# A two-layer attention and feed-forward kernel: a new order of work at the entry into the attention stages

## The chip, the cores and the metric

The kernel runs on one core of a Trainium2 chip. The metric is the device time of one execution in microseconds (us), as the median of several runs. Beside it stands one profiled execution, whose trace gives every instruction of the five engines with its start and length: TensorE (PE; its weight loads as PEld), VectorE (DVE), ScalarE (ACT), GpSimd (POOL) and SyncE (SP, which only issues transfers).

## The reference

Two layers over a sequence of 256 tokens and 1024 features, in float32. Cut to what matters:

```python
for l in range(2):
    h = rmsnorm(x, norm_mix_g[l])                      # mean of squares over 1024 features
    a_qkv, b_q, b_kv, b_gate, merge = split(h @ w_in[l])
    out_a = dilated_mixer(rope(rmsnorm(qa)), rope(rmsnorm(ka)), va)   # 24 heads, three dilations
    k_cmp, v_cmp = compress(...)                       # blocks of 32 tokens, gelu(flat @ w1) @ w2
    out_b = nsa_mixer(rope(rmsnorm(qb)), k_cmp, v_cmp, k_sel, v_sel, k_win, v_win, b_gate)
    gate = sigmoid(merge)
    x = x + (gate_a * (out_a @ w_proj_a[l]) + gate_b * (out_b @ w_proj_b[l])) @ w_out[l]
    h = rmsnorm(x, norm_ffn_g[l])
    g, u = split(h @ w_up[l])                          # 2816 each
    x = x + (silu(causal_dwconv(g, conv_w[l], conv_b[l])) * u) @ w_down[l]
```

The mean of squares is not needed ahead of the products with `w_in` and `w_up`: 1/rms is one factor a token, and the kernel applies it to the results.

## The kernel before

**Units.** All weights come as one stream of units of 128 x 2048 float32 in the order of use. A unit arrives in two halves of 512 KB (`load_half`, L206 on, five buffers `raw`), and each half is split in two parts: ScalarE casts it to `hi` (L238), VectorE subtracts to get `lo` (L239), and every product is three matmuls, hi x hi, lo x hi, hi x lo (`mm3`, L290 to L292; L373 and others in the feed-forward part). So TensorE can begin a half only after ScalarE and VectorE have been through it.

**Entry.** At the start (from L1093) SP issues x in the permuted token order (`xo`, three pieces), the gains and the first two units, interleaved. `feed` (L305 on) scales each of eight 128-feature tiles of x by the gain into a hi and a lo part (ACT L310, DVE L311) and squares it; at the start the first four squares are made by GpSimd (L323), the others by ScalarE (L325), and GpSimd adds them up (L329). VectorE makes the last sum `fin` (L333). The same function feeds the later stages from `x`, where all squares are ScalarE's.

**First three chunks of an attention stage.** `chunk_in` multiplies h by 512 (or 280) columns of `w_in`, in two units (halves kh of the 1024 features) and two token halves t, into two PSUM buffers `acc` of three. The first chunk, `c10`, has the compressed keys and values and half of the others, `c11` (280 columns) the rest and the gates, `bq` the queries. Between the two token halves of `c10`'s second unit stands `rstd_col` (L341 on): two matmuls with `ones` sum `fin` over the features, VectorE scales, GpSimd takes the power -0.5 (L347), VectorE writes two diagonals `dg` (L351). Only with rstd can ScalarE read a chunk out of PSUM, `scaled` (L419): `craw`, `kraw`, `vB`. Each group of heads then runs through `rope_run`, a generator that is stepped by `tick()` between groups of matmuls: squares, sums (L427), power on GpSimd (L378), rotation on VectorE with the tables `tabs` (L436, L437, L440), and `fin`, which copies and transposes (`rd`, L482 and L485). GpSimd makes the tables from `cossin` and `gr` (two instructions at L394, one for `tabc` at L397).

`job_cmp1` (from L787) prepares the compressed blocks: VectorE duplicates (`cdup`, L792), TensorE transposes with the identity (L795), ScalarE copies out of PSUM in natural token order, eight copies a layer (`T`, L802), VectorE adds position terms (`F`, L810). It is begun by a tick inside `c11`.

**Behind the entry.** Nine more chunks follow with the attention steps between them (`job_a`, `job_b`), then projections, and the feed-forward part, where the first unit's matmuls of both output tiles are interleaved, `rstd_col` stands before its 43rd matmul and the row form of rstd before the 25th of the second unit.

**Order.** The code is written as one sequence; a scheduler of the framework sets the final order on each engine's queue, and each engine runs its queue in order.

## Time and profile before

| | |
|---|---|
| median of three runs | 968.22 us (965.47 to 968.27) |
| the profiled execution | 964.59 us |
| its span, first to last instruction | 962.8 us |
| TensorE busy | 936.6 us (97%) |
| VectorE busy | 753.0 us (78%) |
| ScalarE busy | 580.2 us (60%) |
| GpSimd busy | 154.7 us (16%) |
| read from memory | 163.69 MB |

An instruction's row gives its start, its length, the engine, the line, what it writes and reads, and in brackets how long its engine had been idle before it and what ended that. Matmuls overlap: the distance between two starts says what one costs, not its length. The attention stages run from the start to about 240 us and from 484 to about 720 us, the feed-forward parts behind them.

### The profile page before, as it was taken

The numbers are of one execution on the slowest core, as the hardware profiler recorded it, in microseconds if no ns is written. First come the engines' busy times: TensorE is split into PE (matmuls) and PEld (weight loads), VectorE is DVE, ScalarE is ACT, GpSimd is POOL, SyncE is SP. The second block draws the span as 40 slices with busy tenths as digits, with TensorE's granted clock in tenths as the row PEclk, the third lists the DMA queues.
The fourth block names the chain that finished last, engine by engine and source line by source line (L and its number), as shares of the span: only waits on it lengthen the run. The fifth ranks groups of instructions, "written<-read, shape, count | busy, mean of one in ns | idle before, by whom it ended". The sixth has DMA issues, their size and how long they took to land.

```text
span 962.8 us, 18575 instructions
## 1 busy us (share of the span) xinstructions
PE 936.6 (97%) x7122; PEld 848.9 (88%) x7122; DVE 753.0 (78%) x1595; ACT 580.2 (60%) x1186; POOL 154.7 (16%) x179
## 2 busy tenths in 40 slices
PE   6899999999999999999998999999999999999998
PEld 4778887878999999999986787877799999999998
DVE  6898866887679889986478987678876888998742
ACT  6778665666556555555456986466755555655431
POOL 6140211212002111110122301122200111111000
PEclk9999999999999999999999999999999999999999
DMA  7734446525456565666455344554354465666660
GB/s 242 255 132 155 150 157 207 189 88 174 148 162 213 180 210 187 189 196 204 147 168 174 112 151 135 196 196 140 121 180 153 161 217 175 205 197 203 196 209 19
DMA packets 48041, 165.95 MB, mean 172 GB/s; under 512 B 6096, under 2 KB 7632, under 8 KB 47824
## 3 DMA queue, kind: packets, MB, share of 16 engines
q1 hardware_dynamic: 46800, 163.71, 52.1%
q8 instruction: 56, 0.92, 0.4%
q10 hardware_dynamic: 1152, 1.05, 0.3%
q14 instruction: 33, 0.27, 0.1%
HBM read 163.69 MB, written 1.05 MB: 171 GB/s over the span
## 4 chain that ended last, share of the span: by engine, by line
PE 78%; DVE 10%; ACT 6%; issue 2%; POOL 1%; DMA 1%; SPq 0%; DVEq 0%; ACTq 0%; POOLq 0%
PE acc L373 25%; PE acc L290 5%; PE acc L292 5%; PE acc L291 5%; DVE lo L239 4%; PE acc L1082 4%; PE acc L1084 4%; PE acc L1083 4%; PE acc L957 3%; PE att L571 3%; PE acc L959 3%; PE acc L958 3%; PE att L576 2%; PE acc L993 2%; PE acc L994 2%
## 5 line engine op out<-in xcount | busy, mean ns | idle before, releaser
L239 DVE TENSOR_TENSOR lo<-raw,hi 128x1024 fp32r<-128x1024 f32 (+1 forms) x292 | 368.4, 1279 | 51.6 <-ACT hi L238 49.4
L238 ACT CAST hi<-raw 128x1024 fp32r<-128x1024 f32 (+1 forms) x292 | 294.0, 1037 | 150.9 <-PE acc L291 36.9
L373 PE MATMUL acc<-u,hi 128*128 128x256 f32 x1376 | 236.3, 277 | 0.0
L373 PEld LDWEIGHTS acc<-u,hi 128*128 128x128 f32 x1376 | 207.4, 188 | 0.1
L373 PE MATMUL acc<-u,lo 128*128 128x256 f32 x688 | 190.2, 276 | 0.0
L290 PE MATMUL acc<-hi,hT 128*128 128x512 f32 (+1 forms) x384 | 154.0, 401 | 8.7 <-ACT hi L238 8.7
L292 PE MATMUL acc<-lo,hT 128*128 128x512 f32 (+1 forms) x384 | 150.0, 391 | 5.2 <-DVE lo L239 5.1
L291 PE MATMUL acc<-hi,hT 128*128 128x512 f32 (+1 forms) x384 | 148.5, 387 | 0.0
L373 PEld LDWEIGHTS acc<-u,lo 128*128 128x128 f32 x688 | 129.1, 188 | 0.0
L1084 PE MATMUL acc<-act,lo 128*128 128x256 f32 x352 | 97.2, 276 | 0.0
L1082 PE MATMUL acc<-act,hi 128*128 128x256 f32 x352 | 97.2, 276 | 0.0
L1083 PE MATMUL acc<-act,hi 128*128 128x256 f32 x352 | 97.2, 276 | 0.0
L290 PEld LDWEIGHTS acc<-hi,hT 128*128 128x128 f32 x384 | 72.6, 189 | 25.9 <-ACT hi L238 11.1
L292 PEld LDWEIGHTS acc<-lo,hT 128*128 128x128 f32 x384 | 72.4, 189 | 23.6 <-DVE lo L239 9.2
L291 PEld LDWEIGHTS acc<-hi,hT 128*128 128x128 f32 x384 | 72.7, 189 | 12.6 <-issue 0.3
L957 PE MATMUL acc<-hT,hi 128*128 128x256 f32 x256 | 73.4, 287 | 0.0
L959 PE MATMUL acc<-hT,lo 128*128 128x256 f32 x256 | 71.8, 281 | 0.0
L958 PE MATMUL acc<-hT,hi 128*128 128x256 f32 x256 | 71.7, 280 | 0.0
L1084 PEld LDWEIGHTS acc<-act,lo 128*128 128x128 f32 x352 | 66.1, 188 | 0.0
L1082 PEld LDWEIGHTS acc<-act,hi 128*128 128x128 f32 x352 | 66.1, 188 | 0.0
L1083 PEld LDWEIGHTS acc<-act,hi 128*128 128x128 f32 x352 | 66.1, 188 | 0.0
L1054 POOL TENSOR_TENSOR z<-z,rb 128x512 f32<-128x512 f32 x22 | 30.5, 1386 | 203.1 <-DVE z L1053 203.1
(215 smaller groups left out, 1690.2 us busy)
## 6 DMA issues: line engine op xcount, KB each, us to landing
raw<-in_ws_dram SPq DMA_DIRECT2D x300, 512.0 KB, 4.6
raw<-in_ws_dram SPq DMA_DIRECT2D x8, 280.0 KB, 4.2
x<-in_x_dram SPq DMA_DIRECT2D x1, 1024.0 KB, 9.6
out_dram<-x ACTq DMA_DIRECT2D x8, 128.0 KB, 2.7
gr<-in_g_rope_dram SPq DMA_DIRECT2D x2, 384.0 KB, 4.4
masks<-in_mask_dram SPq DMA_DIRECT2D x1, 576.0 KB, 7.6
xo<-in_xo_dram SPq DMA_DIRECT2D x2, 256.0 KB, 4.5
xo<-in_xo_dram SPq DMA_DIRECT2D x1, 512.0 KB, 7.0
```

Of the source, the lines that this page charges most:

```text
L238: A.copy(h, r)
L239: V.tensor_sub(l, r, h.bitcast(F32))
L290: T.matmul(o, a_hi, b_hi, start=first, stop=False)
L291: T.matmul(o, a_lo, b_hi, start=False, stop=False)
L292: T.matmul(o, a_hi, b_lo, start=False, stop=last)
L373: return [lambda a=a: T.matmul(a[0], a[1], a[2], start=a[3], stop=a[4]) for a in todo]
L957: T.matmul(o, hi[:, k, ms], hT[:, 0, k], start=k == 0, stop=False)
L958: T.matmul(o, hi[:, k, ms], hT[:, 1, k], start=False, stop=False)
L959: T.matmul(o, lo[:, k, ms], hT[:, 0, k], start=False, stop=k == 7)
L1082: T.matmul(ps, hi[:, c], act[:, 0, k], start=k == 0, stop=False)
L1083: T.matmul(ps, hi[:, c], act[:, 1, k], start=False, stop=False)
L1084: T.matmul(ps, lo[:, c], act[:, 0, k], start=False, stop=k == NFT - 1)
```

## The change

It rearranges the entries. At the start x and the gains are issued from ACT's queue, the first unit comes in quarters of 256 KB on SP's, each cast and subtracted by itself, and `c10`'s first unit is multiplied quarter by quarter for both token halves. Fourteen matmuls of `ones` with itself, whose result nobody reads, stand first on TensorE. The squares of the first x are made by ScalarE for two tiles at once and added by VectorE; GpSimd has none. In all four places `rstd_col` writes the diagonals with ScalarE; in the attention stages it stands behind all of `c10`, in the feed-forward parts at the fourth matmul of the second unit. In `c11` the token half is the outer loop. The tables are made in pieces, those that the keys need first; `job_cmp1` starts behind `c11`, transposes with two permuted identities, so that the copies out of PSUM are in natural order and two per head pair suffice. The copy `rd` is made before the wait that precedes its transposes and has two buffers of its own.

```diff
+    idle = att()
+    for i in range(14):
+        T.matmul(idle[:, 0:P], ones, ones, start=True, stop=True)
...
-            for c0 in (0, w // 2):
+            step = w // 4 if (i, w // 4) in early else w // 2
+            for c0 in range(0, w, step):
...
+        if src is not x:
+            if m % 2:
+                sq = com.tile([P, 2, S], F32, name="sq2", bufs=2)
+                A.activation(sq, src[:, m - 1:m + 1], AF.Square)
+                if m > 1:
+                    V.tensor_add(sq, sq, sums["acc"])
+                sums["acc"] = sq
+            if m == 7:
+                sums["fin"] = com.tile([P, S], F32, name="fin", bufs=1)
+                V.tensor_add(sums["fin"], sq[:, 0], sq[:, 1])
+            return
...
-            V.tensor_scalar(dg[:, t * P:(t + 1) * P], ident, r[:, 1, t:t + 1], None, op0=ALU.mult)
+            A.activation(dg[:, t * P:(t + 1) * P], ident, AF.Copy, scale=r[:, 1, t:t + 1])
...
-        for a in range(2):
-            G.tensor_tensor(tabs[:, a], cossin[:, a, :, None, :].to_broadcast([P, 2, 5, 64]),
-                            gr[:, a, None, 0:5, :].to_broadcast([P, 2, 5, 64]), op=ALU.mult)
+        def table(k0, k1):
+            for a in range(2):
+                G.tensor_tensor(tabs[:, a, :, k0:k1], cossin[:, a, :, None, :].to_broadcast([P, 2, k1 - k0, 64]),
+                                gr[:, a, None, k0:k1, :].to_broadcast([P, 2, k1 - k0, 64]), op=ALU.mult)
+        table(3, 5)
...
+            if c == "c11":
+                unit(0)
+                for t in range(2):
+                    for kh in range(2):
+                        if t == 0 and kh == 1:
+                            unit(1)
+                        mms(kh, t, range(4), kh == 0, kh == 1)
+                        if kh == 1:
+                            post_fn(t, ps[t])
+                        tick()
+                return
...
+                if c == "c10" and kh == 0:
+                    for k in range(4):
+                        for t in range(2):
+                            mms(0, t, [k], k == 0, False)
+                        if k % 2:
+                            tick()
+                    continue
...
-                        if c == "c10" and t == 0:
+                    if kh == 1 and (c != "c10" or t == 1):
+                        if c == "c10":
                             nrm["col"] = rstd_col()
+                            post_fn(0, ps[0])
                         post_fn(t, ps[t])
...
-                                    dup[:, h, t].rearrange("p a d -> p (a d)"), ident)
+                                    dup[:, h, t].rearrange("p a d -> p (a d)"), perm[:, t])
-                for t in range(2):
-                    src = ps.rearrange("p (h t r i) -> p h t r i", h=2, t=2, r=4)[:, :, t]
-                    for u in range(2):
-                        c0 = t * P + 1 - u
-                        A.copy(by_residue(T2[64 * u:64 * u + 64, :, c0:c0 + P], t), src[64 * u:64 * u + 64])
+                for u in range(2):
+                    r = slice(64 * u, 64 * u + 64)
+                    A.copy(T2[r, :, 1 - u:1 - u + S], ps[r].rearrange("p (h q) -> p h q", h=2))
...
         chunk_in("c10", 512, post_c10)
+        side.append(job_tables())
+        chunk_in("c11", 280, post_c11)
         side.append(job_cmp1())
-        chunk_in("c11", 280, post_c11)
...
-                pg = unit({42: rstd_col}, True)
-                pu = unit({24: lambda: box.update(rb=rstd_row()), 30: lambda: post_g(0, pg)})
+                pg = unit({}, True)
+                pu = unit({3: rstd_col, 27: lambda: box.update(rb=rstd_row()), 33: lambda: post_g(0, pg)})
...
-        nc.sync.dma_start(xo[:, 0:2], xv[:, 0:2])
-        nc.sync.dma_start(gain, g_norm.rearrange("p (a k) -> p a k", k=8))
-        early[0, 0] = load_half(0, 0, UW // 2)
+        A.dma_start(xo[:, 0:2], xv[:, 0:2])
+        A.dma_start(gain, g_norm.rearrange("p (a k) -> p a k", k=8))
+        A.dma_start(xo[:, 2:4], xv[:, 2:4])
+        A.activation(warm, warm, AF.Square)
+        quarters(0, 0)
...
+        prepare(0)
         for m in range(8):
-            if m in (1, 3):
-                if m == 1:
-                    prepare(0)
+            feed(hT, m, 0, False, xo)
+            if m < 4:
                 pend.popleft()[1]()
-            feed(hT, m, 0, False, xo)
```

How the queues change is not visible in these lines alone, since the scheduler orders them. On ScalarE at the start, before (`hT` is the scaled x, `hi` the cast of a weight half, `sq` a square):

```order
L310 ACTIVATE hT<-xo,gain 128x256 x2
L238 CAST hi<-raw 128x1024
L310 ACTIVATE hT<-xo,gain 128x256
L325 ACTIVATE sq<-xo 128x256
L238 CAST hi<-raw 128x1024 x2
```

And now:

```order
L314 ACTIVATE hT<-xo,gain 128x256
L242 CAST hi<-raw 128x512
L326 ACTIVATE sq_125<-xo 128x512
L314 ACTIVATE hT<-xo,gain 128x256 x2
L326 ACTIVATE sq_144<-xo 128x512
L242 CAST hi<-raw 128x1024
L326 ACTIVATE sq_151<-xo 128x512
L242 CAST hi<-raw 128x1024
L242 CAST hi<-raw 128x560 x3
L363 ACTIVATE dg<-ident,rstd 128x128 x2
```

The rows that repeat are left out: four casts of 512 columns stand among eight scalings and four squares of 512 where two casts of 1024 stood, and the last square lies between the second unit's two halves. On GpSimd, from the first instructions that read data to the first power for the heads, before:

```order
L323 TENSOR_TENSOR sq<-xo 128x256
L329 TENSOR_TENSOR acc_101<-acc_101,sq 128x256 x4
L784 MEMSET pad 128x16
L806 MEMSET F 128x32 x2
L347 TENSOR_TENSOR rstd<-rstd,mhalf 128x2
L394 TENSOR_TENSOR tabs<-cossin,gr 128x640 x2
L397 TENSOR_TENSOR tabc<-ropec,gr 128x128
L378 TENSOR_TENSOR rss<-rss,mhalf 128x2 x4
```

And now:

```order
L834 MEMSET pad 128x16
L855 MEMSET F 128x32 x2
L411 TENSOR_TENSOR tabs<-cossin,gr 128x2x128 x2
L411 TENSOR_TENSOR tabs<-cossin,gr 128x2x64 x2
L359 TENSOR_TENSOR rstd<-rstd,mhalf 128x2
L988 TENSOR_TENSOR tabc<-ropec,gr 128x128
L390 TENSOR_TENSOR rss<-rss,mhalf 128x2 x4
```

All six pieces of the tables (two more of 128x2x128 behind those shown) stand ahead of rstd's power, which stood ahead of the tables. They wait for `gr`; on SP's queue, before:

```order
L385 DMA cossin<-in_rope_dram 128x256
L208 DMA raw<-in_ws_dram 128x560
L387 DMA gr<-in_g_rope_dram 128x768
L390 DMA post<-in_pos_dram 128x32
L392 DMA w2t<-in_w_dram 128x256
```

And now:

```order
L400 DMA cossin<-in_rope_dram 128x256
L211 DMA raw<-in_ws_dram 128x560 x3
L996 DMA masks<-in_mask_dram 128x1152
L402 DMA gr<-in_g_rope_dram 128x768
L405 DMA post<-in_pos_dram 128x32
```

Two more halves of `c11` and the masks are issued ahead of `gr`. On VectorE in the second layer, between the last low half of `c11` and the first of `bq`, before:

```order
L239 TENSOR_TENSOR lo<-raw,hi 128x560
L434 TENSOR_TENSOR kraw<-kraw,rss 128x128
L436 TENSOR_TENSOR t_5985<-kraw,tabs 128x128
L810 TENSOR_TENSOR F<-T_6031,post 128x8x15 x4
L437 TENSOR_TENSOR t_6129<-kraw,tabs 128x128
L440 TENSOR_TENSOR t_5985<-t_5985,t_6129 128x128
L239 TENSOR_TENSOR lo<-raw,hi 128x1024
```

And now, the last twelve rows of that stretch:

```order
L453 TENSOR_TENSOR t_5988<-kraw,tabs 128x128
L389 TENSOR_SCALAR rss<-rss 128x2
L454 TENSOR_TENSOR t_6105<-kraw,tabs 128x128
L520 TENSOR_SCALAR gs<-gs 128x24
L451 TENSOR_TENSOR kraw<-kraw,rss 128x128
L444 TENSOR_REDUCE rss<-t_6061 128x2
L457 TENSOR_TENSOR t_5988<-t_5988,t_6105 128x128
L389 TENSOR_SCALAR rss<-rss 128x2
L453 TENSOR_TENSOR t_5993<-kraw,tabs 128x128
L528 COPY rd<-t_5988 128x256
L454 TENSOR_TENSOR t_6112<-kraw,tabs 128x128
L243 TENSOR_TENSOR lo<-raw,hi 128x1024 x2
```

The position sums `F` are gone from here (they come later); the small operations of the first head groups stand ahead of `bq`'s low halves, seventeen or so rows where there were eight.

## Rows read from the trace of the kernel before

**Rows 1.** The page: busy us by engine, and the group of all casts.
```profile
PE 936.6 (97%) x7122; PEld 848.9 (88%) x7122; DVE 753.0 (78%) x1595; ACT 580.2 (60%) x1186; POOL 154.7 (16%) x179
...
L238 ACT CAST hi<-raw 128x1024 fp32r<-128x1024 f32 (+1 forms) x292 | 294.0, 1037 | 150.9 <-PE acc L291 36.9
```

**Rows 2.** What TensorE waits for, whole span: us in total, times, longest.
```profile
PE acc L290 <- ACT hi L238: 8.7, 4, 7.1
PE acc L292 <- DVE lo L239: 5.1, 8, 2.2
PE att L344 <- DVE fin L333: 3.1, 2, 1.6
PE att L485 <- DVE rd L482: 2.6, 2, 1.8
PE att L795 <- DVE cdup L792: 1.9, 2, 1.5
```

**Rows 3.** Windows: busy us of each engine, clock, DMA share, GB/s.
```profile
0.00:5.00 5.00, 0.00 (x0) 0.00 (x0) 0.04 (x1) 2.10 (x4) 1.72 (x11) 1.00 0.50 149
5.00:10.00 5.00, 2.88 (x6) 1.67 (x7) 3.98 (x6) 3.32 (x5) 2.62 (x4) 1.00 0.99 358
50.00:60.00 10.00, 10.00 (x51) 8.11 (x50) 9.67 (x18) 6.18 (x12) 2.61 (x1) 1.00 0.62 212
80.00:90.00 10.00, 10.00 (x74) 9.13 (x73) 10.00 (x37) 8.78 (x25) 0.86 (x1) 1.00 0.43 141
...
240.00:300.00 60.00, 60.00 (x520) 57.86 (x519) 45.71 (x86) 34.13 (x64) 3.98 (x5) 1.00 0.51 164
...
520.00:540.00 20.00, 20.00 (x97) 15.56 (x95) 19.48 (x48) 15.17 (x31) 9.96 (x9) 1.00 0.42 137
```

**Rows 4.** Timeline of entry 1: start, length, instruction, idle before and its end.
```profile
4.42 0.91 ACT L310 ACTIVATE hT<-xo,gain 128x256 fp32r<-128x256 f32 x2 [2.16 <-DMA gain<-in_g_norm_dram]
...
9.37 0.63 PE L291 MATMUL acc<-hi,hT 128*128 128x512 f32 x1
...
9.79 0.63 PE L292 MATMUL acc<-lo,hT 128*128 128x512 f32 x1
...
15.27 2.54 ACT L238 CAST hi<-raw 128x1024 fp32r<-128x1024 f32 x3
...
18.84 1.13 POOL L347 TENSOR_TENSOR rstd<-rstd,mhalf 128x2 f32<-128x2 f32 x1 [2.86 <-DVE rstd L346]
...
19.95 3.11 POOL L394 TENSOR_TENSOR tabs<-cossin,gr 128x640 f32<-128x640 f32 x2
...
20.00 1.54 DVE L348 TENSOR_SCALAR rstd<-rstd 128x2 f32<-128x2 f32 x1 [0.60 <-POOL rstd L347]
...
22.41 0.29 PE L290 MATMUL acc<-hi,hT 128*128 128x280 f32 x1
...
25.77 0.40 PE L292 MATMUL acc<-lo,hT 128*128 128x280 f32 x1 [2.18 <-DVE lo L239]
...
32.70 0.58 PE L290 MATMUL acc<-hi,hT 128*128 128x512 f32 x1
...
40.48 0.47 PE L290 MATMUL acc<-hi,hT 128*128 128x512 f32 x1
```

**Rows 5.** Groups by line, 0 to 60 us: count, busy us, mean ns.
```profile
L810 DVE TENSOR_TENSOR F<-T,post 128x120 f32<-128x120 f32 x8 | 2.4, 354 | 1.4 <-ACT T L802 1.4
...
L419 ACT ACTIVATE vB<-acc,rstd 128x128 f32<-128x128 f32 x4 | 1.5, 370 | 0.0
...
L436 DVE TENSOR_TENSOR t<-kraw,tabs 128x128 f32<-128x128 f32 x4 | 1.1, 285 | 0.0
```

**Rows 6.** Timeline of entry 2, TensorE's three longest waits.
```profile
499.50 0.66 PE L795 MATMUL att<-ident,cdup 128*128 128x128 f32 x4 [1.52 <-DVE cdup L792]
...
508.92 0.50 PE L292 MATMUL acc<-lo,hT 128*128 128x512 f32 x1 [0.72 <-DVE lo L239]
...
514.89 0.44 PE L485 MATMUL att<-ident,rd 128*128 128x128 f32 x2 [1.81 <-DVE rd L482]
```

More of the change, by code (lines that the diff above doesn't have):

```diff
@@ L233, in prepare @@
                 else:
-                    raw = load_half(i, c0, w // 2)
-                c = slice(c0, c0 + w // 2)
+                    raw = load_half(i, c0, step)
+                c = slice(c0, c0 + step)
                 def halve(h=hi[:, c], l=lo[:, c], r=raw):
@@ L321, in feed @@
         sq = sums["acc"] if m == 0 else com.tile([P, S], F32, name="sq", bufs=2)
-        if src is not x and m < 4:
-            G.tensor_tensor(sq, xm, xm, op=ALU.mult)
-        else:
-            A.activation(sq, xm, AF.Square)
+        A.activation(sq, xm, AF.Square)
         if m == 0:
@@ L446, in chunk_in, with unit, mms @@
             ps = [acc(), acc()]
-            for kh in range(2):
-                hi, lo = next_unit(1 if c == "c10" and kh == 1 else 2)
-                hi = hi[:, :4 * ncols].rearrange("p (k n) -> p k n", k=4)
-                lo = lo[:, :4 * ncols].rearrange("p (k n) -> p k n", k=4)
-                for t in range(2):
-                    for k in range(4):
-                        kk = kh * 4 + k
-                        tok = slice(t * P, (t + 1) * P)
-                        mm3(ps[t][:, :ncols], hT[:, 0, kk, tok], hT[:, 1, kk, tok], hi[:, k], lo[:, k],
-                            kh == 0 and k == 0, kh == 1 and k == 3)
-                    if kh == 1:
-                        if c == "c10" and t == 0:
+            un = {}
+            def unit(kh):
+                un[kh] = [z[:, :4 * ncols].rearrange("p (k n) -> p k n", k=4)
+                          for z in next_unit(1 if c == "c10" and kh == 1 else 2)]
+            def mms(kh, t, ks, first, last):
+                for k in ks:
+                    tok = slice(t * P, (t + 1) * P)
+                    mm3(ps[t][:, :ncols], hT[:, 0, kh * 4 + k, tok], hT[:, 1, kh * 4 + k, tok], un[kh][0][:, k],
+                        un[kh][1][:, k], first and k == ks[0], last and k == ks[-1])
+            if c == "c11":
[9 more added lines that the diff above has]
+                return
+            for kh in range(2):
+                unit(kh)
+                if c == "c10" and kh == 0:
+                    for k in range(4):
+                        for t in range(2):
+                            mms(0, t, [k], k == 0, False)
+                        if k % 2:
+                            tick()
+                    continue
+                for t in range(2):
+                    mms(kh, t, range(4), kh == 0, kh == 1)
+                    if kh == 1 and (c != "c10" or t == 1):
+                        if c == "c10":
                             nrm["col"] = rstd_col()
+                            post_fn(0, ps[0])
                         post_fn(t, ps[t])
@@ L489, in fin @@
                 ready["b"] += 1
-            start(rope_run(kraw[:, t, b].rearrange("p (h d) -> p h d", d=64), 3 + b, t, 2, None, fin))
+            start(rope_run(kraw[:, t, b].rearrange("p (h d) -> p h d", d=64), 3 + b, t, 2, None, fin, pre))
         def post_bq(t, ps):
@@ L717, in job_b @@
                 yield
+            yield
             nk = P * (t + 1)
@@ L932, in job_cmp2, with job_tables @@
                 ready["t"] += 1
+        def job_tables():
+            table(2, 3)
+            yield
+            table(0, 2)
+            yield
+            G.tensor_tensor(tabc, ropec, gr[:, :, 5, :], op=ALU.mult)
         chunk_in("c10", 512, post_c10)
+        side.append(job_tables())
+        chunk_in("c11", 280, post_c11)
         side.append(job_cmp1())
-        chunk_in("c11", 280, post_c11)
         nrm["row"] = rstd_row()
@@ L1095, in block_kernel, with quarters @@
         xv = xo_in.rearrange("p (k q) -> p k q", k=8)
-        nc.sync.dma_start(xo[:, 0:2], xv[:, 0:2])
-        nc.sync.dma_start(gain, g_norm.rearrange("p (a k) -> p a k", k=8))
-        early[0, 0] = load_half(0, 0, UW // 2)
+        def quarters(i, h):
+            raw = com.tile([P, UW // 2], F32, name="raw", bufs=5)
+            for j in range(2):
+                c = slice(j * 512, (j + 1) * 512)
+                early[i, h * 1024 + j * 512] = raw[:, c]
+                nc.sync.dma_start(raw[:, c], ws[i][:, h * 1024 + j * 512:h * 1024 + (j + 1) * 512])
+        A.dma_start(xo[:, 0:2], xv[:, 0:2])
[3 more added lines that the diff above has]
+        quarters(0, 0)
         mhalf = com.tile([P, 16], F32, name="mhalf")
         G.memset(mhalf, -0.5)
-        nc.sync.dma_start(xo[:, 2:4], xv[:, 2:4])
-        early[0, UW // 2] = load_half(0, UW // 2, UW // 2)
+        quarters(0, 1)
         nc.sync.dma_start(xo[:, 4:8], xv[:, 4:8])
```

20 lines of the change are left out of this document (13 added, 7 removed).

## The prediction

> **What bounds the kernel now.** I read the page's busy line first: TensorE is busy 97% of the span, VectorE 78%, ScalarE 60% [rows 1]. So the time is TensorE's queue plus the places where it stands still, and the second view to read is the list of what TensorE waits for. Its five longest groups hold 21.4 us, and none lies in the middle of a stage: 8.7 us for the first half of a weight unit (7.1 of it the start), 5.1 us for the second half, 3.1 us for the sum of squares, 2.6 and 1.9 us for the first transposes of the attention stage [rows 2]. With 936.6 us busy, 26 us of the 962.8 are idle, and nearly all belong to four places: the entries into the two attention stages and into the two feed-forward stages. The change touches just these. Third, the windows: in 240 to 300 us TensorE runs 520 matmuls of 256 columns in 60.0 us, 0.115 us each, 0.23 us for one of 512, and nothing else matters. But from 50 to 60 us VectorE is busy 9.67 of 10 us and from 80 to 90 us 10.00, in the second layer 19.48 of 20 [rows 3]. That is the second limit: behind each entry VectorE is full, and a TensorE that comes earlier can be given back there.
>
> **Entry 1, the first unit.** Before, 4.42 us is when ScalarE gets x and the gain; TensorE's first matmul comes at 7.08 and the next are 0.42 us apart (9.37, 9.79), half the later pace: the 1.2 GHz level, though the column of the granted clock says 1.00 there [rows 3, 4]. The change puts x on ACT's queue and the first unit, in quarters, on SP's. Bytes decide, not queues: 0 to 5 us moves 149 GB/s, 5 to 10 us 358 GB/s [rows 3], and x and the first quarter, 256 KB each, now share the first stretch, so x lands 256 KB / 358 GB/s = 0.7 us later, at 5.1. Were the two queues two roads, it would still be 4.4. The Trainium skill (DMA: Bandwidth & Descriptors, Rules for kernel authors) says that spreading transfers over issuing engines buys no bandwidth, only issue time; by it 5.1 stands, and by the other reading the sum below would be 0.7 us larger.
>
> From 5.1 us ScalarE owes, up to the second unit's high halves, eight scalings of 256 columns (0.91 for two [rows 4]: 3.6), four casts and four squares of 512, and two casts of 1024 (1.04 each [rows 1]: 2.1). A width of 512 is not in the trace; between 0.46 and 1.04 the line through both widths gives 0.65, so 5.2. Together 10.9: done at 16.0. Before, the same two casts begin at 15.27, three taking 2.54, so they end near 17.3 [rows 4]. VectorE subtracts the low half 1.2 later, 17.2, and twelve matmuls of 0.23 (2.8) end the chunk at 20.0; the column sum now follows all of it, 0.3 more: 20.3, against 22.41, when the next chunk begins before [rows 4]. Gain 2.1. VectorE gets three sums of 512 columns and two permuted copies for this, some 2.4 by the same line; they stand beside ScalarE's list, for which VectorE waits anyway, and what goes is ten GpSimd operations and ScalarE's waits for them. ScalarE sets the stretch, so the fourteen idle matmuls and the early pace are worth nothing by themselves: with 0.13 us, what 280 columns cost at 0.23 for 512, as lower end and four times that (4-byte operands in two passes, half the pace) as upper, they run from 1.0 to between 2.8 and 8.3 us, I take 6.6; even from 8.3 the first unit's 24 products are through by 13.8, just before the second unit's first high half. Beyond 8.3 each microsecond would cost one.
>
> **Entry 1, the second chunk.** Three things swap. (a) The six tables on GpSimd stood behind rstd and now stand ahead of it, and they need gr, which SP issues behind the 576 KB of masks. About 5.1 MB come up to gr; 0.75 MB pass by 5 us, the rest at 358 GB/s takes 12.2 us: 17.2. The tables take 3.1 us [rows 4]. Meanwhile VectorE has low halves to make. At 20.00 its instruction on two columns took 1.54 us, until the first table had ended [rows 4]: the two engines lock each other out. So I add 1.5 us for two subtractions to the tables, which then end at 21.8. The Trainium skill (SBUF — State Buffer, Who interferes with whom) calls the port that the two share an exclusive lock, held for a whole instruction, and counts instructions with two inputs in SBUF among those that need it; by it the 1.5 stands, and if only the form seen at 20.00 were locked, the sum would be 1.5 larger. Behind the tables rstd takes 1.1 [rows 4], then dg, dg, craw, kraw, vB on ScalarE 0.37 each [rows 5]: 24.8. Only then is the PSUM buffer free for the second token half. TensorE has 18 matmuls of 0.13 to do, until 22.7, and waits 2.1. Before it waited 2.18 at 25.77 [rows 4]: nothing won. (b) Thirty matmuls are left, 3.9, the row sum 0.25, and two low halves that stand behind a dozen small VectorE operations of 0.285 [rows 5], some 1.5 of waiting: the third chunk begins at 30.4, against 32.70 [rows 4], 2.3 earlier; the eight transposes for the compressed keys (0.9, taken at 0.115 each) are still owed. (c) In the third chunk before needs 7.8 us to 40.48 for 24 products and four transposes, after 24 x 0.23 and twelve transposes, 6.9 in all: 37.3. Entry 1 gains 3.2; bounds below.
>
> **The full VectorE behind it.** The eight sums for the compressed blocks, 2.4 us of VectorE [rows 5], stood before 35 us and now come around 42 to 50, and TensorE can't use a microsecond that VectorE doesn't have. At worst 2.4 of the 3.2 goes back; at best the later wait for rd, 0.8 of the 2.6 [rows 2], goes too and everything idle in this stretch with it, 6.5. I leave 3.2: ScalarE has four copies there instead of eight, and GpSimd's squares no longer lock VectorE in the first 15 us. The earlier copy of the rotated keys and the finished duplicates only change places in that list.
>
> **Entry 2.** Before waits 1.52 at 499.50, 0.72 at 508.92 and 1.81 at 514.89 [rows 6], with 0.4 for a high half 4.45 together. gr is early here, so rstd costs 0.5, the power between 0.7 and 1.1, and five ScalarE instructions, 1.85: 3.1 to 3.5 us, and the 24 matmuls of the first token half, 3.1, cover it but for a few tenths. But the low halves of the third chunk now stand behind 17 operations of 0.285, 4.85, with two waits for GpSimd's power in them (about 0.5); counted from the first chunk's end that is 3.6 + 4.85 + 0.5 + 1.2 = 10.15 us, and TensorE is there after 0.4 + 48 x 0.127 + 0.25 + 0.9 = 7.7. New wait 2.45, net 2.0. Bounds: 4.45 if those 17 fit elsewhere, -0.5 if the waits for GpSimd in that list come to 3.
>
> **Feed-forward entries.** rstd_col stands nine matmuls later in TensorE's queue; the sum of squares is no earlier. 9 x 0.115 = 1.03 of each 1.55 us wait is filled [rows 2, 3]. Twenty-four matmuls, 2.8 us, still separate it from the row sum; rstd with the diagonal on ScalarE needs about 2.6. Two entries: 2.1, from 1.0 (the diagonal late behind two casts) to 3.1.
>
> **The sum.** 3.2 + 2.0 + 2.1 = 7.3 us. The profiled execution took 964.59, 1.8 more than its span, so it would take 957.3; the three runs have a median of 968.22, and I predict 968.2 - 7.3 = 960.9. The ends of the terms give 1.0 - 0.5 + 1.0 = 1.5 and 6.5 + 4.45 + 3.1 = 14: 966.7 and 954.2.
>
> **Rivals.**
> - VectorE takes the entries back: of entry 1 only 1.0 is left, of entry 2 nothing, of the feed-forward 2.1. 968.2 - 3.1 = 965.1. For it, the full windows [rows 3]; against it, that VectorE no longer waits for GpSimd's sums at the start.
> - TensorE alone counts: tables out of the way, no new waits, 13 us, 955.2. For it, that the waits before sit where work was moved away; against it, ScalarE's 10.9 us list.
> - It does not do what it says: after 5 us the traffic runs at 270 GB/s and not at 358, gr comes at 21 and not at 17.2, and rstd, the buffer and the second token half all come 3.8 later; entry 2 gives nothing. Gain 3.2 - 3.8 + 2.1 = 1.5, less a little for VectorE: 967. For it, masks ahead of gr; against it, that nothing else on SP stands between.
> - Slower: the scheduler's new order of ScalarE through the attention steps. Eight steps of the windowed and four of the dilated heads in two layers, 24, each let TensorE wait for a copy of transposed probabilities. Half a microsecond each is 12 us, 968.2 - 7.3 + 12 = 972.9; it decides from 0.43 us a step (7.3 + 2.9 over 24). Against it: before, TensorE waits almost nowhere in these steps; the entries hold the list [rows 2].
>
> **How the numbers follow.** Forecast 0.61, with its own range 957.5 to 964.5; VectorE 0.18; TensorE alone 0.09; not as said 0.06; slower 0.06. About 0.3%, 2.9 us, is what a measurement of this kernel tells from no change, so faster means under 965.3: 0.61 + 0.09 and just over half of the VectorE case, 0.80. Same: the rest of it and the case not as said, 0.14. Slower 0.06. The range 954.5 to 966.0 leaves out half of the TensorE case, the case not as said and the slower one, with a little of the others.
>
> **What would show it.** In the changed profile: first matmul of the first chunk between 6 and 7 us, 0.23 apart; the second chunk at 20, its second token half after a wait of about 2 us that ends with ScalarE; the rstd power on GpSimd near 22, right behind the tables; the third chunk near 30; in layer two no wait for the compressed keys' copies but one of 2 to 2.5 us for a low half of the third chunk; in the feed-forward two waits of 0.5 us for the sum of squares. Wrong it would be if rstd starts before the tables end by much, if the second token half of the second chunk does not wait, or if TensorE's waits between 60 and 240 us grow past 2 us in all.

## The result, and the profile after

The changed kernel takes 962.04 us (median of 6 runs, 960.51 to 963.14), the one before 967.13 in the same rounds (6 runs). The ratio is 0.9945, with a 95% interval of 0.9932 to 0.9958: a gain of 4.1 to 6.6 us. The profiled execution took 961.09 us, its span 959.3, which is 3.5 less than before. The time lies in the forecast range, 1.1 us from the forecast. The gain was forecast as 7.3, and for the profiled execution 957.3.

The page's line of busy time, which answers to [rows 1]. VectorE has 7.5 us less to do, GpSimd 7.8:

```profile
PE 940.0 (98%) x7150; PEld 856.2 (89%) x7150; DVE 745.5 (78%) x1594; ACT 577.6 (60%) x1188; POOL 146.9 (15%) x177
```

What TensorE waits for over the whole span, against [rows 2] (us in total, times, longest). The sum of squares, the copies for the compressed keys and the rotated keys are gone from the list. New are the queries' low parts (qS), a copy in the windowed heads (sc) and the last block of u:

```profile
PE acc L296 <- DVE lo L243: 4.9, 8, 2.1
PE acc L294 <- ACT hi L242: 3.3, 2, 2.4
PE att L778 <- DVE qS L300: 2.3, 2, 1.5
PE att L644 <- ACT sc L646: 1.6, 2, 1.2
PE acc L385 <- DVE u L315: 1.4, 2, 0.8
PE att L190 <- POOL ones L186: 1.1, 1, 1.1
```

The windows that answer to [rows 3]: busy us and instructions of TensorE, weight loads, VectorE, ScalarE and GpSimd, then granted clock, DMA share, GB/s. From 50 to 60 us VectorE is as full as before, and now TensorE stands idle 1.45 us there; before it did not.

```profile
50.00:60.00 10.00, 8.55 (x44) 7.03 (x43) 9.78 (x19) 7.78 (x16) 1.75 (x2) 1.00 0.49 161
80.00:90.00 10.00, 10.00 (x75) 8.90 (x74) 9.79 (x32) 8.37 (x23) 0.00 (x0) 1.00 0.38 121
240.00:300.00 60.00, 60.00 (x518) 57.85 (x517) 45.53 (x87) 33.98 (x64) 3.35 (x5) 1.00 0.51 163
520.00:540.00 20.00, 18.87 (x93) 15.23 (x92) 19.72 (x52) 13.02 (x28) 7.98 (x9) 1.00 0.42 133
```

TensorE's timeline through entry 1, which answers to [rows 4]: start, length, instruction, and in brackets the idle time before it and what ended it. The fourteen idle matmuls stand as 28 rows.

```profile
1.05 4.74 PE L190 MATMUL att<-ones 128*128 128x128 f32 x28 [1.05 <-POOL ones L186]
8.23 0.51 PE L294 MATMUL acc<-hi,hT 128*128 128x512 f32 x1 [2.44 <-ACT hi L242]
...
15.10 0.51 PE L294 MATMUL acc<-hi,hT 128*128 128x512 f32 x1 [0.83 <-ACT hi L242]
...
21.66 0.38 PE L294 MATMUL acc<-hi,hT 128*128 128x280 f32 x1
...
25.82 0.40 PE L296 MATMUL acc<-lo,hT 128*128 128x280 f32 x1 [2.12 <-DVE lo L243]
29.69 0.40 PE L296 MATMUL acc<-lo,hT 128*128 128x280 f32 x1 [0.36 <-DVE lo L243]
...
31.46 0.58 PE L294 MATMUL acc<-hi,hT 128*128 128x512 f32 x1
...
58.18 0.97 PE L778 MATMUL att<-kS,qS 128*128 128x512 f32 x4 [1.45 <-DVE qS L300]
```

The idle matmuls end at 5.8, and then TensorE waits for data. The second chunk starts at 21.66 and the third at 31.46, before at 22.41 and 32.70. GpSimd shows why the second chunk stops at 25.82:

```profile
20.38 3.63 POOL L411 TENSOR_TENSOR tabs<-cossin,gr 128x256 f32<-128x256 f32 x6 [18.66 <-DMA raw<-in_ws_dram]
23.97 0.71 POOL L359 TENSOR_TENSOR rstd<-rstd,mhalf 128x2 f32<-128x2 f32 x1
```

VectorE waits for that power, and the low half that TensorE needs stands behind it in VectorE's queue:

```profile
21.84 0.16 DVE L358 TENSOR_SCALAR rstd<-att 128x2 f32<-128x2 f32 x1 [1.93 <-PE att L356]
24.71 0.41 DVE L360 TENSOR_SCALAR rstd<-rstd 128x2 f32<-128x2 f32 x1 [2.72 <-POOL rstd L359]
25.04 0.73 DVE L243 TENSOR_TENSOR lo<-raw,hi 128x560 fp32r<-128x560 f32 x1
```

**Where the gain stays.** TensorE's products of weights can be counted on both traces, 5856 rows on each. The lead of a run is the start of the n-th product in the trace before, minus its start in that run's trace. Each lead comes from one execution. Programs that are the same up to a point differ there by up to 0.7 us (1.24, 1.42 and 1.93 at the third chunk in three of them), so smaller differences are not read. In the second attention stage seven of these runs (the changed kernel, x_first, ffn_hooks_before, gr_early, no_idle, ffn_k7 and tables_behind_rstd) have the same code, and it adds 0.5 to 3.1 us to their leads; a single figure of that stage says little inside this range.

| lead over before, us | third chunk | attention 1, at 142 us of before's time | end of feed-forward 1 (484) | end of attention 2 (706) | last product (959) | ratio to before, 95% interval |
|---|---|---|---|---|---|---|
| the changed kernel | 1.24 | 0.89 | 0.35 | 3.03 | 3.37 | 0.9945 (0.9932 to 0.9958) |
| x_first | 1.56 | -0.15 | 0.22 | 3.29 | 3.69 | 0.9954 (0.9938 to 0.9970) |
| ffn_hooks_before | 1.93 | 1.52 | 0.74 | 2.68 | 1.12 | 0.9959 (0.9944 to 0.9974) |
| no_sums | 1.71 | 2.47 | 2.04 | 6.02 | 6.37 | 0.9918 (0.9904 to 0.9932) |
| no_yield | 1.52 | 2.03 | 1.80 | 3.84 | 4.14 | 0.9928 (0.9915 to 0.9941) |
| gr_early | 1.10 | -0.39 | -0.46 | 2.47 | 2.87 | 0.9965 (0.9950 to 0.9980) |
| no_idle | 2.01 | 1.63 | 1.40 | 3.55 | 3.20 | 0.9947 (0.9927 to 0.9967) |
| cmp_early | 1.24 | 0.15 | -0.12 | 3.31 | 3.10 | 0.9940 (0.9922 to 0.9959) |
| ffn_k7 | 1.42 | 1.12 | 2.12 | 2.61 | 2.62 | 0.9924 (0.9905 to 0.9944) |
| tables_behind_rstd | 4.52 | -0.29 | -0.49 | 0.55 | 0.33 | 0.9972 (0.9960 to 0.9985) |
| k7_no_yield | 1.98 | 2.50 | 2.87 | 5.17 | 5.45 | 0.9921 (0.9909 to 0.9934) |
| k7_no_yield1 | 1.73 | 2.22 | 2.58 | 5.63 | 6.25 | 0.9918 (0.9905 to 0.9932) |
| blocks_late | 0.78 | 1.96 | 2.06 | 6.91 | 7.62 | 0.9886 (0.9867 to 0.9905) |

In the changed kernel's row, attention 1 gives 0.9, its feed-forward stage loses 0.5, attention 2 gives 2.7 and the last stage 0.3: 3.4 in all. Between the first two columns it is 3.2 us at 40 us of before's time, 0.8 at 60, 3.3 at 77 and 106, for a moment 5.7 at 81; a part of this comes and goes because transposes and scores, which are not counted, stand in another order. By 142 it is 0.9.

### The profile page after: what moved, and what is told of

It reads as the page before. It is cut to its first block, busy times and chain, and to the rows that moved or that the text cites. A ratio compares the mean times of both kernels' runs of the same rounds, so it can differ in the third digit from the quotient of the medians.

```text
span 959.3 us, 18628 instructions
## 1 busy us (share of the span) xinstructions
PE 940.0 (98%) x7150; PEld 856.2 (89%) x7150; DVE 745.5 (78%) x1594; ACT 577.6 (60%) x1188; POOL 146.9 (15%) x177
## 4 chain that ended last, share of the span: by engine, by line
PE 76%; DVE 12%; ACT 6%; issue 2%; DMA 2%; POOL 1%; ACTq 0%; DVEq 0%
PE acc L385 25%; PE acc L296 5%; PE acc L294 5%; PE acc L295 5%; DVE lo L243 5%; PE acc L1139 4%; PE acc L1140 4%; PE acc L1141 4%; PE att L620 3%; PE acc L1014 3%; PE acc L1016 3%; PE acc L1015 3%; PE att L625 2%; ACT pt L713 2%; PE acc L1050 1%
## 5 line engine op out<-in xcount | busy, mean ns | idle before, releaser
L243 DVE TENSOR_TENSOR lo<-raw,hi 128x1024 fp32r<-128x1024 f32 (+2 forms) x294 | 368.2, 1270 | 52.2 <-ACT hi L242 50.2
L242 ACT CAST hi<-raw 128x1024 fp32r<-128x1024 f32 (+2 forms) x294 | 294.2, 1031 | 150.0 <-PE acc L295 47.8
```

What stands on the lines that cost most here:

```text
L242: A.copy(h, r)
L243: V.tensor_sub(l, r, h.bitcast(F32))
```

## The experiments

Each differs from the changed kernel by the edit shown.

**x_first.** Is the late first scaling the loads' doing, and what is it worth?

```diff
-        A.dma_start(xo[:, 0:2], ...); A.dma_start(gain, ...); A.dma_start(xo[:, 2:4], ...)
+        nc.sync.dma_start(xo[:, 0:2], ...); nc.sync.dma_start(gain, ...)
         quarters(0, 0)
+        nc.sync.dma_start(xo[:, 2:4], ...)
```

> x's first pair, the gain and the second pair go back to SP's queue, x and gain ahead of the quarters; all else as in the changed kernel. In the order of SP's issues gr then stands ahead of the second chunk's weights. Theory A (the late start is the loads' doing: 1.8 MB share the first stretch and the gain lands at 7.16 us instead of 4.42): the first scaling at 4.4 to 5.0, the first product at 5.5 to 6.5 instead of 8.23, the second unit's high half 1.5 to 2.7 earlier than 15.10, the tables end before 20 instead of 24.0, rstd at 21 to 22 instead of 23.97, and 1.5 to 3 us of it stay to the end: 959 to 960.5. Theory B (VectorE is full from 36 to 58 us and takes it back): the third chunk starts 2 to 3 us earlier all the same, but at 145 us less than 0.5 us is left, and the time is within 0.7 us of the changed kernel's.

The first scaling is at 4.42 again and the power of rstd at 19.93, but TensorE gained nothing from either. The idle matmuls held it until 7.04, and the last half of x, now behind more on the same queue, reached ScalarE at 12.15. So the second unit's high half came at 15.96, later than 15.10. This is TensorE at that place:

```profile
15.96 0.50 PE L294 MATMUL acc<-hi,hT 128*128 128x512 f32 x1 [2.78 <-ACT hi L242]
...
18.00 0.63 PE L294 MATMUL acc<-hi,hT 128*128 128x512 f32 x1
18.43 0.63 PE L295 MATMUL acc<-hi,hT 128*128 128x512 f32 x1
18.85 0.63 PE L296 MATMUL acc<-lo,hT 128*128 128x512 f32 x1
```

And the same trace's window, with the granted clock third from the right:

```profile
17.00:21.00 4.00, 4.00 (x14) 3.27 (x13) 2.36 (x4) 0.33 (x2) 4.00 (x5) 0.57 0.71 214
```

After a wait of 2.78 us the products are 0.43 us apart, the 1.2 GHz level, for seven products (1.5 us), and the second chunk starts at 23.6 instead of 21.66. Theory A is right that the loads set the first scaling, and wrong on its worth. Theory B is right on the time, but a lead of 1.56 at the third chunk was not the 2 to 3 that it had to take back.

**no_idle.** Are the fourteen idle matmuls worth anything?

```diff
-    for i in range(14):
-        T.matmul(idle[:, 0:P], ones, ones, start=True, stop=True)
```

> The fourteen idle matmuls at the start are left out; all else as in the changed kernel. The forecast (ScalarE sets the stretch, the early pace is worth nothing by itself): the first products stand 0.42 us apart instead of 0.23, the second unit starts 1 to 3 us later than 15.10, but the wait for rstd behind the tables (2.28 us at 25.82) gives the same, and the third chunk starts within 0.5 us of the changed kernel; time within 0.5 us. Rival (the clock counts): the half pace lasts through the first unit and part of the second, the first chunk ends 2 to 4 us later than 21.3, later than the tables, and 1.5 to 3 us of it stay: 963.5 to 965.

The first products come at the slow pace:

```profile
7.99 0.80 PE L291 MATMUL acc<-hi,hT 128*128 128x512 f32 x1 [7.99 <-ACT hi L239]
8.58 0.63 PE L292 MATMUL acc<-hi,hT 128*128 128x512 f32 x1
9.01 0.63 PE L293 MATMUL acc<-lo,hT 128*128 128x512 f32 x1
```

Still the second chunk starts within 0.2 us of the changed kernel's, the third no later, and the time is the same (0.9947 beside 0.9945). The forecast's step stands: the stretch is not TensorE's.

**gr_early.** Do the tables hold the second chunk because gr comes late?

```diff
+        load_gr(gr0[0], 0)      # own tile, issued behind the second unit's weights
         prepare(0)
```

> Layer one's gr gets a tile of its own and is issued right behind the second unit's weights, before the constants and the second chunk's weights; the masks come behind those. All else as in the changed kernel. Theory T (the tables, which wait for gr until 20.38 us, hold rstd until 23.97, and the wait of 2.28 us at 25.82 hangs on that): the tables run between 13 and 18 us, rstd's power comes within 1.2 us of the end of the first chunk (22 to 22.6), the wait at 25.82 falls under 0.6, and the third chunk starts 1.5 to 2.5 us earlier than 31.4. Of this 0.7 to 2 us last to the end. Rival (VectorE from 36 us on takes it back, or GpSimd's tables now lock VectorE while it makes the low halves of the first two units): the second unit's low half comes 0.5 to 1.5 later than 16.58, and the time is within 0.7 us of the changed kernel's.

The rival came true. The tables now run beside VectorE's work on the first two units, GpSimd here:

```profile
15.08 5.32 POOL L413 TENSOR_TENSOR tabs<-cossin,gr 128x256 f32<-128x256 f32 x6
```

and VectorE at the same time:

```profile
16.08 1.23 DVE L394 COPY perm<-ident 128x128 f32<-128x128 f32 x2
17.18 1.49 DVE L243 TENSOR_TENSOR lo<-raw,hi 128x1024 fp32r<-128x1024 f32 x1
18.59 1.21 DVE L328 TENSOR_TENSOR sq<-sq,sq 128x512 f32<-128x512 f32 x1
19.73 1.76 DVE L243 TENSOR_TENSOR lo<-raw,hi 128x1024 fp32r<-128x1024 f32 x1
```

In the changed kernel the same instructions take 0.41, 1.22, 0.69 and 1.22 us, and the tables 3.63. So both engines get longer, and the second unit's low half comes at 18.72 instead of 16.58. In the second chunk nothing waits any more, but the lead at 142 us is -0.39: 1.3 worse. The Trainium skill (SBUF — State Buffer, Who interferes with whom) says that a VectorE instruction with two inputs in SBUF contends with a GpSimd instruction that reads SBUF; these rows agree for the subtractions and sums.

**tables_behind_rstd.** The opposite: all tables behind rstd, as in the kernel before.

```diff
-        nc.sync.dma_start(gr, ...)       # layer one
-        table(3, 5)
         chunk_in("c10", 512, post_c10)
+        load_gr(); table(3, 5)           # gr lands behind three halves of the third chunk
         ...
         chunk_in("bq", 512, post_bq)
+        nc.sync.dma_start(masks, mask_c); nc.sync.dma_start(x, ...)
```

> In layer one gr is loaded behind the third chunk's first three halves, so that all six tables stand behind rstd on GpSimd, as in the kernel before; masks and x are issued where they are or later. All else as in the changed kernel. Theory T (in the changed kernel rstd waits for the tables until 23.97 us, VectorE stands idle from 20 to 24.7 behind rstd with the second chunk's low half queued after it, and TensorE's wait of 2.28 us at 25.82 hangs on that low half): rstd's power at 22 to 22.7 us, the wait at 25.82 under 0.8, the third chunk 1.3 to 2 us earlier than 31.4. The tables then run from about 25 us and lengthen VectorE's instructions beside them by 1 to 2 us in all. If VectorE has room for that, 0.7 to 2 us last to 145 us. Rival (VectorE takes it back: the ropes of the keys, which need the tables, come 3 us later into the full stretch): the lead at the third chunk is gone by 60 us, the wait for the queries' low parts grows past 2 us, and the time is the same or up to 2 us slower.

Theory T is shown as far as it goes: rstd's power at 21.84, no wait in the second chunk, the third chunk 3.3 us earlier than in the changed kernel (lead 4.52). Then the tables meet the third chunk's low halves. On VectorE two of them take 3.14 us, where two without GpSimd take 2.36, and they start late:

```profile
28.96 0.81 DVE L456 TENSOR_TENSOR kraw<-kraw,rss 128x128 f32<-128x128 f32 x1 [0.81 <-POOL rss L390]
29.70 3.14 DVE L243 TENSOR_TENSOR lo<-raw,hi 128x1024 fp32r<-128x1024 f32 x2
```

TensorE waits for the first of them, and behind that wait its clock falls, here its timeline:

```profile
31.50 0.68 PE L296 MATMUL acc<-lo,hT 128*128 128x512 f32 x1 [2.50 <-DVE lo L243]
31.97 0.63 PE L294 MATMUL acc<-hi,hT 128*128 128x512 f32 x1
32.40 0.63 PE L295 MATMUL acc<-hi,hT 128*128 128x512 f32 x1
```

The lead at 142 us is -0.29. Some 1.6 us of that are the clock's (eight products 0.43 apart instead of 0.23). Without them the lead would be near the changed kernel's 0.89, so the place of the tables would be worth nothing that lasts; this is argued from the trace, no run has this order with the full clock. Each of the three places tried leaves TensorE one wait of 2 to 2.5 us (2.12 in the changed kernel, 2.00 in gr_early, 2.50 in this run). By the ratios the run is 2.6 us slower than the changed kernel: 1.2 are gone at 142 us, and 1.6 more in the second attention stage (1.0 won there instead of 2.7), whose code is the same.

**no_sums.** Does the full VectorE take entry 1's lead?

```diff
-                        V.tensor_tensor(Fv[:, 8 * jh:8 * jh + 8, h, 0:15], tv[...], post[...], op=ALU.add)
+                G.memset(Fv[:, :, :, 0:15], 0.0)
```

> Leaves out the eight sums per layer that make the compressed blocks (they hold zeros, written by GpSimd), some 0.27 us of VectorE each in a row, 2.2 us a layer; all else as in the changed kernel. Theory B (VectorE, full from 36 to 58 us, sets when the queries' low parts are there): TensorE's wait of 1.61 us at 58.18 falls under 0.4, and 1 to 2.2 us a layer are won, 2 to 4 in all: 958 to 960. Theory C (the lead goes because the windowed heads' jobs start one step later and the order of the jobs is another): within 0.7 us of the changed kernel.

It does. What TensorE waits for from 36 to 145 us, qS no longer in the list:

```profile
PE att L644 <- ACT sc L646: 1.1, 1, 1.1
PE att L778 <- DVE mxb L785: 0.3, 1, 0.3
```

The lead at 142 us is 2.47; three runs that are the same program up to there have 0.89, 1.12 and 1.52. So 2.2 us less on VectorE give 1 to 1.6 in layer one, and about as much in layer two (from 2.04 to 6.02, the changed kernel from 0.35 to 3.03). The time falls by 2.6 us (0.9918 beside 0.9945).

**no_yield.** Or is it the order of the windowed heads' jobs?

```diff
             while ready["b"] < 6:
                 yield
-            yield
             nk = P * (t + 1)
```

> Takes out the one extra step by which the change lets the windowed heads' jobs start later; all else as in the changed kernel. Theory B (VectorE): the first scores stand one step earlier in TensorE's queue and the queries' low parts are no earlier, so the wait at 58.18 grows from 1.6 us, and the time is within 0.7 us or up to 1.5 us slower. Theory C (the order of the jobs): 1 to 2 us faster.

This counts too, by its trace: 2.03 at 142 us, while its 2.0 us in layer two lie within the range of the runs with the same code there. By the ratios 1.6 us are won, with intervals that overlap. Theories B and C are not rivals here: the wait for qS is as long in sum (2.2 us in four waits instead of 2.3 in two), those for sc are gone, and one of 1.2 for a copy of the queries (qkT) is new.

**cmp_early.** Would VectorE's sums cost less where they were before?

```diff
+        side.append(job_cmp1())
         chunk_in("c11", 280, post_c11)
-        side.append(job_cmp1())
```

> The job that makes the compressed blocks starts one chunk earlier, in the second chunk, as in the kernel before; all else as in the changed kernel. Theory B (the eight sums, 2.2 us, fall into the stretch from 36 to 58 us in which VectorE is full; earlier it has 2.6 us free from 24 to 36): the sums come before 38 us, the wait of 1.61 us at 58.18 falls under 0.7, the third chunk starts up to 1 us later because two copies and four transposes stand there, and 0.5 to 1.5 us a layer are won. Rival (the copies and sums only change places, and the low halves of the third chunk's weights come later by what they take): the third chunk starts 1 to 2 us later, the wait at 58.18 stays over 1 us, and the time is the same or up to 2 us slower.

No difference that can be measured (0.9940). The wait for qS at 58.37 is 1.09 instead of 1.45, and one of 0.76 for the keys' copies is back at 35.56. The rival's reading, that work only changes places, fits layer one. In layer two this run wins 3.4 us, no less than the changed kernel, and waits 0.4 us for the keys' copies where the kernel before waits 1.52; so the later place of that job does not show as a source of the second stage's gain.

**ffn_hooks_before.** Is the wait at the feed-forward entry one for the sum of squares?

```diff
-                pg = unit({}, True)
-                pu = unit({3: rstd_col, 27: ..rstd_row.., 33: ..post_g..})
+                pg = unit({42: rstd_col}, True)
+                pu = unit({24: ..rstd_row.., 30: ..post_g..})
```

> The feed-forward stages get the places of before back: rstd's column after 42 of the first unit's 48 products, the row after 24 of the second unit's, the gate's work after 30. All else as in the changed kernel. The forecast's term (9 products filled the wait for the sum of squares in each of two stages): 2.1 us slower, 1.0 to 3.1. The theory after the two traces (products 42 to 47 need the last block of u, which is ready 0.4 us before the sum of squares, so the column was only first in a wait that the products would have had): 0 to 0.8 us slower for both stages together, with the wait again put down to the sum of squares, 1.4 to 1.8 us a stage.

In the first feed-forward stage the places make no difference (it loses 0.8 us of lead, the changed kernel 0.5). In the second it loses 1.6, where the changed kernel wins 0.3. That is not the wait, which is 1.46 us, 0.1 less than before had there, but what follows it in TensorE's clock:

```profile
780.00:784.00 4.00, 3.45 (x20) 3.45 (x21) 1.87 (x5) 1.66 (x4) 0.70 (x1) 0.71 0.57 198
```

Seventeen products there are 0.1 us further apart than the others, 1.7 us in all. Without it the places are worth 0.2 to 0.3 us: the expectation from the two traces, 0 to 0.8, holds, and the forecast's 2.1 doesn't; of the waits for the sum of squares, expected at 1.4 to 1.8 us, the first is only 0.9. By the ratios the two kernels can't be told apart.

**ffn_k7.** Cover the last block of u instead.

```diff
+                pg, early_g, late_g = halves(0); run(early_g)     # 42 products each: blocks 0 to 6
+                pu, early_u, late_u = halves(1); run(early_u + late_g)
+                rstd_col(); run(late_u)
```

> In both feed-forward stages the first gate unit and the first up unit run their first 42 products each before either takes the products with the last block of u; the column of rstd follows the twelve last ones' first half, its row stands in the next unit. All else as in the changed kernel. Theory F (what TensorE waits for at each entry, 1.12 and 0.73 us, is the last block of u, and 42 products of another unit, 4.8 us, cover it): both waits vanish, and 1 to 2 us are won if the second unit's halves are there in time. Rival (ScalarE and VectorE make the second unit's halves in that very time, behind the work on u): a wait of 1 us or more for hi or lo of the second unit comes instead, and the time is within 0.7 us or slower.

Theory F holds for the entries: no wait for u is left, and up to their last gate and up product the first stage adds 1.8 us to the lead and the second 1.7. But the down products behind them now wait for the gated activations (`act`), once in each stage, which they did not in the changed kernel:

```profile
PE acc L1161 <- DVE act L300: 0.9, 2, 0.6
```

Behind the second of these waits they also run 0.118 us apart instead of 0.113, up to 924 us. At the end of the stages 1.0 and 0.0 us are left. The second attention stage gives 0.5, where the changed kernel has 2.7; TensorE waits 1.3 us for qS there instead of 0.8, and 0.7 for a copy of the queries (qkT) is new. Whether this is more than chance was not settled: k7_no_yield1, with the same code there, wins 3.1. By the ratios 2.0 us are won (0.9924). The profiled execution, 961.81, is the slowest of the six, whose median is 959.47, so its leads may be too small.

**k7_no_yield, k7_no_yield1, blocks_late.** Versions put together from what had worked.

> The entries of the feed-forward stages as in ffn_k7, and the windowed heads' jobs without the extra step in both layers, as in no_yield. If the two are independent, their gains add: 2.0 us (ffn_k7, by the ratios) and 1.7 us (no_yield), 958.5 or so beside 962.3 for the changed kernel. Rival (the second attention stage keeps only a part of any lead: with ffn_k7 it entered 2.1 us ahead of the kernel before and left 2.6 ahead, with the changed kernel 0.35 and 3.0): 960 to 961.

> As k7_no_yield, but the extra step is left out in layer one alone, where no_yield won 1.2 us of lead by its trace; in layer two it lost 0.6 against the changed kernel. If that is a property of the layer: 0.3 to 1 us faster than k7_no_yield. If it is chance of where the jobs fall: within 0.7 us of it, either way.

They take 958.99 and 958.40 us. By the ratios they are 2.3 and 2.6 us below the changed kernel, less than the sum of the two gains (3.6), and not told apart from each other. The extra step's loss in layer two is thus not shown to belong to the layer.

```diff
+        def job_blocks():               # transposes, copies and sums, from a buffer of their own
...
+            if c == 2:
+                active.append(job_blocks())
             chunk_in(c, 512, post_a(c))
```

> k7_no_yield1 with the transposes, copies and eight sums that make the compressed blocks moved behind the second chunk of the dilated heads (80 to 95 us in layer one; they are first read near 100), where VectorE is busy 17.4 of 20 us instead of all of the time; the copies of the keys stay early, in a buffer of their own. Theory B (VectorE, full from 36 to 58 us, sets when the windowed heads start): as with no_sums, which won 1.5 us of lead a layer by leaving the sums out, the wait for the queries' low parts falls under 0.7 in all and 1.5 to 3 us are won over k7_no_yield1: 955.5 to 957. Rival (VectorE has no room there either, 60 to 100 us being 92% busy: the sums delay the maxima of the scores or the first use of the blocks): within 0.7 us of k7_no_yield1, with a new wait for the blocks or for the copies of probabilities.

956.71 us, ratio 0.9886 (0.9867 to 0.9905): the best kernel, faster than before by 11 us, by the ratios 3.1 us under k7_no_yield1, with intervals that touch, and 5.7 under the changed kernel, with no new wait of size. Over the whole span the wait for qS is down to this:

```profile
PE att L779 <- DVE qS L300: 0.3, 1, 0.3
```

Its own gain shows in layer two (4.9 us of lead won in that attention stage, k7_no_yield1 3.1). In layer one it shows none: 1.96 beside 2.22 at 142 us, after a wait of 2.33 at 25.65 with a clock of 0.70 from 28 to 32 us behind it.

## Why the prediction was right, and which steps failed

- **What bounds the kernel** was right: TensorE plus four entries, and a full VectorE behind them.
- **The full VectorE behind entry 1** is one of the two steps that failed by 2.3 us. The forecast saw the eight sums move into the full stretch and priced them at up to 2.4 us given back, then left 3.2. TensorE did lead by 3.2 at 40 us and kept 0.9, nearly the 1.0 of the rival (which was wrong on entry 2). no_sums shows that 2.2 us less work for VectorE bring 1 to 1.6 of it back, no_yield that an earlier start of the windowed heads' jobs brings 0.5 to 1.1. That the move of the sums took the lead is not shown: cmp_early has them earlier, as before, and leads by 0.15 at 142.
- **The feed-forward entries** are the other: forecast 2.1, found -0.2 by the leads, 0.45 of it lost behind the first entry at a slower pace (last section). The failing words are "9 x 0.115 = 1.03 of each 1.55 us wait is filled". Six of these nine products need the last block of u, which VectorE finishes 0.4 us before the sum of squares. TensorE in the changed kernel, at the place of [rows 2]'s third line:

```profile
307.78 0.39 PE L385 MATMUL acc<-u,hi 128*128 128x256 f32 x1 [0.85 <-DVE u L315]
```

ffn_k7, which fills the wait with products that need nothing new, gets 1.8 and 1.7 at the entries and keeps 1.0 and 0.0 to the ends of the stages.
- **Entry 1, the first unit**: x was to land at 5.1, and its first 256 KB did so, 4.2 us after their issue at 0.73. But ScalarE began at 7.16, for the gain came later. Here are the gain's transfer, with its size and the us from its issue at 1.18 to its landing, and ScalarE's row:

```profile
gain<-in_g_norm_dram ACTq DMA_DIRECT2D x1, 16.0 KB, 5.9
7.16 0.51 ACT L314 ACTIVATE hT<-xo,gain 128x256 fp32r<-128x256 f32 x1 [3.50 <-DMA gain<-in_g_norm_dram]
```

The forecast let only x and the first quarter share the first stretch and did not count the gain, whose 16 KB are issued behind 256 KB of x and beside the other quarters. ScalarE's list was shorter than feared (a width of 512 takes 0.52 from start to start where I had 0.65), so the second chunk came at 21.66 against 20.3. The idle matmuls' worth, nothing, was right.
- **Entry 1, the second chunk**: forecast a wait of 2.1 us behind tables and rstd, found 2.12. The size is luck in part: gr landed near 20.4 and not at 17.2 (SP issued it only at 13.82: three weight transfers ahead of it took SP 4.5 us, waiting for VectorE's low halves), the tables were not lengthened, and what ended the wait was VectorE's low half behind rstd, not ScalarE. The third chunk came at 31.46 against 30.4.
- **Entry 2**: forecast 2.0, found 2.7 for the attention stage. The waits for the copies `cdup` and `rd` are gone, as forecast. The wait for the third chunk's low half is 1.1 us and not 2.45; 1.2 and 0.8 for sc and qS came behind it. No run takes back the early copy `rd`, the permuted transposes, the quarters or the new squares, so which of them brings this gain, or the first chunk's, stays open; shown is only that the place of `job_cmp1`, the idle matmuls and the places in the feed-forward parts bring no measurable part of it.
- **The sum**: 0.9 - 0.5 + 2.7 + 0.3 = 3.4 us between the profiled executions, 5.1 between the medians, for 7.3. The time came within 1.1 us in part by luck: the three runs' median of 968.22, from which I counted, is 1.1 above that of the six. For the profiled execution, 957.3 was forecast and 961.09 measured.
- Of the signs named for "wrong", TensorE's waits between 60 and 240 us stayed under 2 us (1.5 in the list of waits, before 0.9); the wait that counted stood at 58.18, just ahead of the window I had named.

## What to carry to other kernels

Before moving an instruction out of a wait, look what the work behind it waits for: if that is ready a moment earlier, only work that needs neither fills the wait. Then look at what comes behind those products: a wait that is filled at the entry can come back there in part, as in ffn_k7. Behind an entry where a second engine is full for tens of microseconds, most of a lead of the first engine may be lost; look for a later stretch with room and move the second engine's work there (here this showed in layer two, not in layer one). Where two engines lengthen each other's instructions, as GpSimd's tables and VectorE's subtractions did here, try the place where one of them waits anyway: of the three places for the tables it had the best time (0.9945 beside 0.9965 and 0.9972, the first two with intervals that overlap).

## What the runs showed of the hardware

- The clock falls behind some waits and not behind others of the same length. After 2.44 us at 8.23 and 2.12 at 25.82 the changed kernel kept 1.00, as the kernel before did after 1.55 at 783. After 2.30 at 8.57 gr_early was granted 0.57 from 8 to 12 us, ffn_hooks_before 0.71 behind 1.46 at 780.55, tables_behind_rstd 0.62 behind 2.50. In the fourteen profiled executions it happened to seven, for 3 to 4 us each. In the first unit it is hidden behind ScalarE (no_sums and ffn_k7 had it there and still lead by 1.71 and 1.42 at the third chunk); elsewhere it costs 1.5 to 1.7 us, a third of this change's gain. A wait that is taken away may be worth that much more than its length, and a comparison of two single traces may be off by as much.
- In no_idle the first ten products run 0.43 us apart while the column of the granted clock says 1.00, as before the change [rows 3, 4].
- At a granted clock of 1.00 products of 256 columns run 0.113 us apart in some stretches and 0.118 in others. In the changed kernel the slow pace lasts from 296 to 338 us, before from 302 to 323 with gaps; this is the 0.45 us that its first feed-forward stage loses between 318 and 334. What sets it stays open.
- A copy with one input was lengthened by GpSimd too: the two of 128x128 took 1.23 us beside the tables and 0.41 alone.
